# One broadcast VectorE multiply per output tile in an expert-dispatch kernel that copies and scales rows

## The chip, the cores and the metric

The kernel runs on one core of a Trainium2 chip. The metric is the device time of the whole program in microseconds (us); each run is one execution, and the median of the runs is taken. Durations inside the kernel come from one profiled execution.

Of the core's engines three issue or compute here: VectorE (DVE in the profile) and ScalarE (ACT) multiply, and SyncE (SP), ScalarE and GpSimd (POOL) issue transfers. The transfers themselves are carried by 16 DMA engines, which all three queues share. HBM is the memory off the core; SBUF is the memory on the core, with 128 partitions.

## The reference

Each of 16 x 1024 tokens has a row of 512 fp32 numbers and two weights. The output holds the row twice, once times each weight. The expert indices aren't used.

```python
batch, seq, hidden, n_experts, k = 16, 1024, 512, 8, 2

def reference(x, expert_indices, expert_weights):
    x_expanded = x[:, :, np.newaxis, :].repeat(k, axis=2)
    weights = expert_weights[..., np.newaxis]
    return (x_expanded * weights).astype(np.float32)
```

The input is 33.5 MB and the output 67.1 MB, all fp32; every input row is read once and every output row written once.

## The kernel before

**Tiles.** The 16,384 tokens are 128 tokens per partition over 128 partitions. They are cut into six load tiles: five of 24 tokens per partition (6.29 MB, 48 KB in each partition) and a last one of 8 (2.10 MB). The output of a load tile is made in pieces of `TO = 12` tokens per partition: two outputs for each of the first five load tiles (6.29 MB each) and one of 8 tokens (4.19 MB) for the last. So there are six loads, numbered 0 to 5, and eleven outputs, numbered 0 to 10.

**Buffers.** The pool of `x_tile` has two buffers, and so has the pool of `o_tile`. A third output can be made only when the first of the two before it has landed in HBM, and a third load can be issued only when the first tile has been read by its last multiply. All weights have one tile, `w_tile` (256 numbers per partition), filled at the start by six small loads from GpSimd's queue (line 54).

**Queues.** Loads are issued from ScalarE's queue (`load`, line 75), the first two at the very start and load i+2 behind the multiplies of load tile i (line 109). ScalarE also multiplies, and its instructions run in the order in which they are issued, so a load stands behind ScalarE's multiplies of its tile. Outputs are issued from SyncE's queue (line 105), which does nothing else; each waits for the multiplies that fill its buffer.

**Multiplies.** For each token and each of its two weights one instruction multiplies a block of 128 partitions x 512 numbers by one weight per partition. With `c` the column of the weight, the ones with `c % 3 == 2` go to ScalarE (line 90) and the others to VectorE (line 96): in a 12-token output 8 of the 24 on ScalarE and 16 on VectorE. The order on each engine is the order of the program; a tile framework puts in the waits.

Of the kernel before, what the change touches and what calls it, by code (L numbers as in the profile page):

```python
# [1 line left out]

# [4 lines left out]


@with_exitstack
def kernel(  # L10
    ctx: ExitStack,
    tc: tile.TileContext,
    x: bass.AP,
    expert_indices: bass.AP,
    expert_weights: bass.AP,
    out: bass.AP,
):
    nc = tc.nc

    batch, seq, hidden = x.shape  # L20
    k = expert_weights.shape[-1]
    P = nc.NUM_PARTITIONS
    ntok = batch * seq
    assert ntok % P == 0
    A_TOTAL = ntok // P

    f32 = mybir.dt.float32
    row = k * hidden
    TX = 24
    TO = 12  # L30

    groups = [[24], [24], [24], [24], [24], [8]]
    assert sum(sum(g) for g in groups) == A_TOTAL

    xf = x.rearrange("b s h -> (b s) h")
    of = out.rearrange("b s k h -> (b s) (k h)")
    wf = expert_weights.rearrange("b s k -> (b s) k")

    w_pool = ctx.enter_context(tc.tile_pool(name="w_pool", bufs=1))
    x_pool = ctx.enter_context(tc.tile_pool(name="x_pool", bufs=2))  # L40
    o_pool = ctx.enter_context(tc.tile_pool(name="o_pool", bufs=2))

    w_tile = w_pool.tile([P, A_TOTAL * k], f32)

    def rows(of_all, done, T):
        return of_all[done * P : (done + T) * P, :].rearrange(
            "(p a) n -> p (a n)", a=T
        )

    weights = []  # L50
    for group in groups:
        weights.append((sum(n for _, n in weights), sum(group)))
    for at, T in weights:
        nc.gpsimd.dma_start(out=w_tile[:, at * k : (at + T) * k], in_=rows(wf, at, T))  # L54

    tiles = []
    done = 0
    for group in groups:
        T = sum(group)
        a0 = 0  # L60
        for n in group:
            tiles.append((done, T, a0, n))
            a0 += n
        done += T

    loaded = []

    def load(i):
        if i >= len(tiles):
            return  # L70
        done, T, a0, n = tiles[i]
        x_tile = x_pool.tile([P, TX * hidden], f32)
        cols = rows(xf, done, T)[:, a0 * hidden : (a0 + n) * hidden]
        for lo, hi in [(0, P)]:
            nc.scalar.dma_start(out=x_tile[lo:hi, : n * hidden], in_=cols[lo:hi, :])
        loaded.append(x_tile)

    for i in range(2):
        load(i)
    for i, (done, T, a0, n) in enumerate(tiles):  # L80
        x_tile = loaded[i]
        outr = rows(of, done, T)
        for t in range(n):
            if t % TO == 0:
                o_tile = o_pool.tile([P, TO * row], f32)
            for kk in range(k):
                c = (done + a0 + t) * k + kk
                o = t % TO * row + kk * hidden
                if c % 3 == 2:
                    nc.scalar.mul(  # L90
                        out=o_tile[:, o : o + hidden],
                        in_=x_tile[:, t * hidden : (t + 1) * hidden],
                        mul=w_tile[:, c : c + 1],
                    )
                    continue
                nc.vector.tensor_scalar(  # L96
                    out=o_tile[:, o : o + hidden],
                    in0=x_tile[:, t * hidden : (t + 1) * hidden],
                    scalar1=w_tile[:, c : c + 1],
                    scalar2=None,  # L100
                    op0=mybir.AluOpType.mult,
                )
            if (t + 1) % TO == 0 or t + 1 == n:
                at = t // TO * TO
                nc.sync.dma_start(  # L105
                    out=outr[:, (a0 + at) * row : (a0 + t + 1) * row],
                    in_=o_tile[:, : (t + 1 - at) * row],
                )
        load(i + 2)

# [1 line left out]
_INS = ['x', 'expert_indices', 'expert_weights']  # L112
_OUTS = [((16, 1024, 2, 512), 'float32')]


# [23 lines left out]
```

## Time and profile before

| | value |
|---|---|
| time, median of 3 runs | 241.27 us (240.94 to 241.39) |
| time of the profiled execution | 241.42 us |
| its span, first to last instruction | 239.7 us |
| bytes read from and written to HBM in it | 33.69 MB and 67.11 MB |
| VectorE multiplies (line 96) | 171, mean 479 ns, 16 of them back to back in 6.43 us |
| ScalarE multiplies (line 90) | 85, mean 708 ns, 8 of them back to back in 5.01 us |
| first load: issued, first multiply | 0.73 us, 19.33 us |
| first output issued | 25.84 us |
| last output issued, last landing seen | 218.79 us, 238.36 us |

The span counts from the first instruction to the last on the core. The profiled execution's own time is 1.7 us above its span. Below, a digit row cuts the span in 40 slices and gives the busy share of each in tenths (9 is 90% or more). In the chain of work that ended last, each piece is followed back to what released it; its lines hold the start, the length and the work. In a timeline line the first two numbers are start and length in us, then engine, line, operation, tiles and count, and in brackets the idle time before it and what ended it. A "q" behind an engine's name is its queue. A multiply's length is longer than the distance to the next one, since successive ones overlap.

### The profile page before, as it was taken

The page shows a single profiled execution, that of the slowest core. Times are in us where ns is not written, and L with a number is a line of the kernel's source. Part 1 is how long each engine was busy: PE and PEld are TensorE (multiplying, and loading weights), DVE is VectorE, ACT ScalarE, POOL GpSimd, SP SyncE. Part 2 cuts the span into 40 slices and gives each one's busy share as a digit, 9 for nine tenths or more (in the row PEclk, how much of TensorE's full clock was granted, in tenths as well). Part 3 has the DMA queues.
Part 4 walks back from the last instruction along what each step waited for, and adds up shares of the span by engine and source line. Part 5 has one row for each costly group of instructions (what it writes and reads, how often), then busy time and mean ns, then how long its engine had stood idle before and what let it go on. Part 6 is the DMA issues. An engine that isn't in the chain of part 4 may idle for free.

```text
span 239.7 us, 366 instructions
## 1 busy us (share of the span) xinstructions
DVE 68.6 (29%) x171; ACT 54.5 (23%) x86; POOL 3.5 (1%) x10
## 2 busy tenths in 40 slices
DVE  0007930000820820820055028003705406425000
ACT  0007900000800800800052016003505206122000
POOL 5000000000000000000000000000000000000000
DMA  7999999999999999999999999999999999999894
GB/s 262 468 442 408 402 394 402 492 410 410 451 451 402 436 468 410 418 476 418 402 459 443 402 443 453 418 427 459 418 402 459 407 459 451 394 451 459 388 432 175
DMA packets 2642, 100.81 MB, mean 421 GB/s; under 512 B 368, under 2 KB 464, under 8 KB 464
## 3 DMA queue, kind: packets, MB, share of 16 engines
q1 hardware_dynamic: 1584, 67.11, 64.7%
q10 hardware_dynamic: 864, 33.55, 33.2%
q0 software_dynamic: 192, 0.13, 0.2%
q14 instruction: 2, 0.02, 0.0%
HBM read 33.69 MB, written 67.11 MB: 421 GB/s over the span
## 4 chain that ended last, share of the span: by engine, by line
DMA 75%; DVE 15%; issue 0%; DVEq 0%; SPq 0%
DMA out_dram<-o_tile 67%; DVE o_tile L96 15%; DMA x_tile<-in_x_dram 8%; DVEq L134 0%; DVEq L96 0%; SPq L105 0%
## 5 line engine op out<-in xcount | busy, mean ns | idle before, releaser
L96 DVE TENSOR_SCALAR o_tile<-x_tile,w_tile 128x512 f32<-128x512 f32 x171 | 68.6, 479 | 150.1 <-DMA out_dram<-o_tile 130.8
L90 ACT ACTIVATE o_tile<-x_tile,w_tile 128x512 f32<-128x512 f32 x85 | 53.2, 708 | 143.7 <-DMA out_dram<-o_tile 143.7
L90 ACT ACT_TABLE_LOAD x1 | 1.3, 1283 | 19.3 <-DMA x_tile<-in_x_dram 19.3
L54 POOL DMA_DIRECT2D w_tile<-in_expert_weights_dram x6 | 3.3, 557 | 0.8 <-PEq L134 0.8
L123 POOL MEMSET const-float32-0.0<- 128x1 f32 x1 | 0.1, 99 | 0.2 <-issue 0.2
L123 POOL MEMSET const-bfloat16-1.0<- 128x1 bf16 x1 | 0.1, 102 | 0.0
L123 POOL MEMSET const-float32-1.0<- 128x1 f32 x1 | 0.1, 99 | 0.0
L123 POOL MEMSET const-uint8-127<- 128x1 uint8 x1 | 0.1, 99 | 0.0
## 6 DMA issues: line engine op xcount, KB each, us to landing
out_dram<-o_tile SPq DMA_DIRECT2D x10, 6144.0 KB, 34.0
x_tile<-in_x_dram ACTq DMA_DIRECT2D x5, 6144.0 KB, 33.9
out_dram<-o_tile SPq DMA_DIRECT2D x1, 4096.0 KB, 19.6
x_tile<-in_x_dram ACTq DMA_DIRECT2D x1, 2048.0 KB, 23.5
w_tile<-in_expert_weights_dram POOLq DMA_DIRECT2D x5, 24.0 KB, 14.8
w_tile<-in_expert_weights_dram POOLq DMA_DIRECT2D x1, 8.0 KB, 22.7
```

What stands on the lines that cost most here:

```text
L54: nc.gpsimd.dma_start(out=w_tile[:, at * k : (at + T) * k], in_=rows(wf, at, T))
L90: nc.scalar.mul(out=o_tile[:, o : o + hidden], in_=x_tile[:, t * hidden : (t + 1) * hidden], mul=w_tile[:, c : c + 1],)
L96: nc.vector.tensor_scalar(out=o_tile[:, o : o + hidden], in0=x_tile[:, t * hidden : (t + 1) * hidden], scalar1=w_tile[:, c : c + 1], scala ...
L123: nc = _bacc.Bacc("TRN2", target_bir_lowering=False, num_devices=1)
```

## The change

The loop over the two weights and its two kinds of instruction are taken out. Instead, when the last token of an output tile is reached, one VectorE `tensor_tensor` makes the whole output: its first input is the `x_tile` rows of these tokens, each repeated for the two weights by a step of 0; its second input is the weights of these tokens, each repeated over 512 numbers by a step of 0; its output is the whole `o_tile`, 12 x 2 x 512 = 12,288 numbers per partition (8,192 in the last output). ScalarE multiplies nothing any more and only issues the loads. Buffers, tile sizes, the queues and the places of the loads and of the outputs in the program stay.

```diff
         for t in range(n):
             if t % TO == 0:
                 o_tile = o_pool.tile([P, TO * row], f32)
-            for kk in range(k):
-                c = (done + a0 + t) * k + kk
-                o = t % TO * row + kk * hidden
-                if c % 3 == 2:
-                    nc.scalar.mul(
-                        out=o_tile[:, o : o + hidden],
-                        in_=x_tile[:, t * hidden : (t + 1) * hidden],
-                        mul=w_tile[:, c : c + 1],
-                    )
-                    continue
-                nc.vector.tensor_scalar(
-                    out=o_tile[:, o : o + hidden],
-                    in0=x_tile[:, t * hidden : (t + 1) * hidden],
-                    scalar1=w_tile[:, c : c + 1],
-                    scalar2=None,
-                    op0=mybir.AluOpType.mult,
-                )
             if (t + 1) % TO == 0 or t + 1 == n:
                 at = t // TO * TO
+                m = t + 1 - at
+                c = (done + a0 + at) * k
+                shape = [P, m, k, hidden]
+                nc.vector.tensor_tensor(
+                    out=o_tile[:, : m * row].rearrange(
+                        "p (t k h) -> p t k h", k=k, h=hidden
+                    ),
+                    in0=x_tile[:, at * hidden : (t + 1) * hidden]
+                    .rearrange("p (t o h) -> p t o h", o=1, h=hidden)
+                    .to_broadcast(shape),
+                    in1=w_tile[:, c : c + m * k]
+                    .rearrange("p (t k o) -> p t k o", k=k, o=1)
+                    .to_broadcast(shape),
+                    op=mybir.AluOpType.mult,
+                )
                 nc.sync.dma_start(
                     out=outr[:, (a0 + at) * row : (a0 + t + 1) * row],
                     in_=o_tile[:, : (t + 1 - at) * row],
```

## The prediction

> **What bounds the kernel now.** I read the page's busy shares, slices and chain first, then the chain in order of time and the timeline of the last tiles, to see what covers what.
>
> ```profile
> span 239.7 us, 366 instructions
> DVE 68.6 (29%) x171; ACT 54.5 (23%) x86; POOL 3.5 (1%) x10
> DMA  7999999999999999999999999999999999999894
> HBM read 33.69 MB, written 67.11 MB: 421 GB/s over the span
> DMA 75%; DVE 15%; issue 0%; DVEq 0%; SPq 0%
> ```
>
> VectorE works 29% of the span and ScalarE 23%, while the DMA engines are full in nearly every slice. The chain puts 15% on VectorE, but the DMA row shows no dip in those stretches: while VectorE fills one output buffer, the other one is on its way out. So the transfers bound the kernel, and VectorE matters only if it takes longer than what the DMA engines still have queued.
>
> How long that cover is shows where no load is in flight:
>
> ```profile
> 199.80 6.42 DVE L96 TENSOR_SCALAR o_tile<-x_tile,w_tile 128x512 f32<-128x512 f32 x16 [11.20 <-DMA out_dram<-o_tile]
> 206.29 12.84 SPq L105 DMA_DIRECT2D out_dram<-o_tile  x2
> 214.28 4.45 DVE L96 TENSOR_SCALAR o_tile<-x_tile,w_tile 128x512 f32<-128x512 f32 x11 [8.06 <-DMA out_dram<-o_tile]
> ```
>
> I number the eleven outputs 0 to 10 and the six loads 0 to 5. VectorE starts at 199.80 because output 7 has landed, and at 214.28 because output 8 has. Between them only outputs move: one output of 6.29 MB takes 14.48 us alone, 434 GB/s. Output 9 is issued at 206.29, so today there is about 8 us to spare. Where a load moves too, the cover is longer: in the whole timeline VectorE starts at 97.05 and 122.43 on two successive landings with load 3 beside them, 25.4 us.
>
> The start and a handover:
>
> ```profile
> 19.22 0.03 issue
> 19.25 0.02 DVEq L96
> 19.27 0.06 issue
> 19.33 6.43 DVE o_tile L96 x16
> 25.76 0.02 issue
> 25.78 0.02 SPq L105
> 25.80 0.04 issue
> 25.84 34.83 DMA out_dram<-o_tile
> 60.66 0.03 issue
> 60.69 0.05 DVEq L96
> 60.74 0.05 issue
> 60.79 6.43 DVE o_tile L96 x16
> ```
>
> Landing to first VectorE work is 0.13 us (60.66 to 60.79), VectorE's end to the issue of the output 0.08 us (25.76 to 25.84). From the trace's records of single packets come two more: load 0 is issued at 0.73 and its first packet starts at 1.75, so 1.02 us; its last packet ends at 18.67 and the landing is seen at 19.22, so 0.55 us.
>
> **The change, part by part.** *Removed from ScalarE:* 85 multiplies and a table load, 54.5 us. They lie beside VectorE's work: in each tile 8 x 626 ns (8 in 5.01 us) against VectorE's 16 x 402 ns (16 in 6.43 us), and VectorE ends last. Nothing comes off the path.
>
> *Loads on ScalarE's queue:* the same six, in the same order. Loads 2 to 5 still wait for the last reader of their x_tile, which was VectorE and stays VectorE (issues at 85.43 on SP and 85.44 on ACT in one go). Only their time moves with C, below. SP's outputs and POOL's six weight loads keep their order and number.
>
> *VectorE:* 16 instructions per 12-token tile become one with 12,288 results; in the 8-token tile one with 8,192. Its length C replaces 6.43 us. No row shows such an operation, so I bound it. Today's VectorE pace for all 24 rows is 24 x 0.402 = 9.65 us. At ScalarE's pace it is 24 x 0.626 = 15.0 us. Twice the VectorE time, since two streams are read where one was, is 19.3 us. Between: an instruction's fixed part, paid once now, may be near the 0.10 us of the 128x1 memsets in the trace; 0.30 us of stream doubled is 24 x 0.60 = 14.4 us. I take the mean of 9.65, 14.4 and 15.0, 13.0 us, and keep 9.65 and 19.3 as ends. VectorE's busy time would be 10.67 tiles x 13.0 = 139 us, 58% of the span: the engine is still not the bound by its sum.
>
> [...] No run here shows the operation yet.
>
> *What C does at a handover.* When output j lands, VectorE makes output j+2, and the DMA engines live on output j+1 and on any load. Load and odd output are issued together, so when an even output is made (2, 4, 6, 8) both are in flight, 25 us or more of cover: free. When an odd one is made (3, 5, 7, 9), the load is about done and only the even output, 14.48 us, is left: four thin handovers. Output 10 takes 8/12 x 13.0 = 8.7 us under output 9's 14.48: free. At the start output 0 is made from 19.33 with only load 1 in flight: a fifth one. Output 1 is made while output 0 moves: it is issued about 45.4, output 0 ends about 48: free.
>
> The gap at a thin handover: from the landing it takes 0.13 + C + 0.08 + f until new packets move, with f the delay from issue to first packet; the cover ends 14.48 - 0.55 = 13.93 after the landing. Gap = C + f - 13.72. For f I have 1.02 us (load 0, idle engines) and, from the packet records, 3.65 us (load 3, issued at 85.44, first packet 89.09, behind other packets). At a thin handover the engines run dry, so I take 1.2, near the first. With C = 13.0 the gap is 0.48 us; break-even is C = 12.7 at f = 1.02. The start by itself: output 0 issued at 19.33 + 13.0 + 0.08 = 32.4, first packet 33.6; load 1 ends about 18.67 + 14.48 = 33.15: gap 0.45, the same. After a gap the wait is for the next landing: everything behind moves by it, for the DMA engines never get idle time back.
>
> Sum: 5 x 0.48 = 2.4 us. The profiled execution took 241.42 us (span 239.7 and 1.7 around it): 243.8 us. It lies 0.15 above the median of the three runs, less than I can tell; 0.2% (0.5 us) is what a measurement here tells from no change.
>
> **The rivals.**
> *The cover holds, no loss.* If C is below 12.7 us no gap opens at any thin handover, and the time stays 241.3. For it: today's pace gives 9.65; also, a load packet that trails behind its output adds cover. Against it: two streams are read. A gain can go with it: outputs start 6.6 us later, so the end of load 1 runs unmixed. The slices from 18 to 42 us moved 408, 402, 394 and 402 GB/s against 434 later; if all of that came back, 24 us x 32/434 = 1.8 us, so 239.6 at best. Only part of it can, since the first slices are slow with loads alone.
> *VectorE sets the pace of the thin handovers.* At C = 14.4 the gap is 1.9 us, the sum 241.4 + 9.4 = 250.8; at 15.0 it is 2.5 and 253.8; at 19.3 it is 6.8 and 275. For it: ScalarE needs 626 ns per row with one stream; against: VectorE does one row in 402.
> *A slow restart.* With f = 3.65 and C = 13.0 each gap is 2.9 us: 241.4 + 14.6 = 256. For it: three loads had to wait so long; against: they stood behind packets of another queue, which at a dry handover are gone. A middle f of 2.2 gives 1.5 each, 248.8.
> *The change doesn't do what it says:* the instruction order of the changed kernel shows eleven TensorTensor on VectorE and no multiply on ScalarE, so I give this nothing.
>
> **How the numbers follow.** Small gaps (C about 13, f 1.0 to 1.8): 0.60, 242 to 247, likeliest 243.8. Cover holds: 0.22, of it 0.14 within 0.2% and 0.08 faster. VectorE sets the pace: 0.12. Slow restart: 0.06. Slower: 0.60 + 0.12 + 0.06 = 0.78. The range goes from 240.8, no change and a little of the gain, to 250.5, which takes in the middle restart and C up to 14.4.
>
> **What would show it.** In the profile after: VectorE's one line with 11 instructions near 13.0 us for the 12-token ones, busy near 139 us; ScalarE near nothing; the first output issued near 32.4 us; the DMA row below 9 near 33 us and before the issues of outputs 3, 5, 7 and 9 (near 90, 134, 178 and 212 us) and full elsewhere; one output alone still 14.5 us. A mean under 12.7 us with a full DMA row would prove the first rival; gaps at every landing the second; a dry stretch well over 1.2 us between issue and first packet the third. The prediction is wrong if the slices between the handovers move less than 434 GB/s, which no term here has.

## The result, and the profile after

| | before | after |
|---|---|---|
| time, median | 241.31 us (4 runs, 240.94 to 241.39) | 247.45 us (4 runs, 246.77 to 247.66) |
| ratio to before, 95% interval | | 1.0256 [1.0239, 1.0273] |
| profiled execution, its span | 241.42 us, 239.7 us | 247.66 us, 245.9 us |

The change makes the kernel 2.6% slower. The direction was forecast; the forecast of 243.8 us priced the loss at 2.4 us, and it is 6.1 us.

The page of the changed kernel: its span, busy times, the DMA row (a slice is 6.1 us here), the GB/s moved in each slice, the chain's shares, and the multiply's group (busy, mean ns, idle before).

```profile
span 245.9 us, 108 instructions
DVE 138.2 (56%) x11; POOL 3.5 (1%) x10
DMA  7999999999999988899899999999998989989895
GB/s 265 487 408 405 472 400 400 384 376 408 456 416 432 464 384 264 384 440 456 384 472 424 384 344 424 456 440 424 424 432 341 469 384 426 512 384 512 384 426 256
DMA 63%; DVE 30%; issue 0%; DVEq 0%
L91 DVE TENSOR_TENSOR o_tile<-x_tile,w_tile 128x12288 f32<-128x12288 f32 (+1 forms) x11 | 138.2, 12570 | 91.1 <-DMA out_dram<-o_tile 71.9
```

VectorE is busy twice as long, 138.2 us for 68.6, and still only 56% of the span; its share of the chain went from 15% to 30%. The DMA row now has dips, and the slice from 92 to 98 us moved 264 GB/s. That is around the issue of output 3, one of the odd outputs.

The timeline there; ahead of it stands the line of fill 4 from the kernel before:

```profile
97.05 6.43 DVE L96 TENSOR_SCALAR o_tile<-x_tile,w_tile 128x512 f32<-128x512 f32 x16 [11.69 <-DMA out_dram<-o_tile]
```

```profile
61.95 46.74 SPq L103 DMA_DIRECT2D out_dram<-o_tile  x3
80.83 12.96 DVE L91 TENSOR_TENSOR o_tile<-x_tile,w_tile 128x12288 f32<-128x12288 f32 x1 [18.91 <-DMA out_dram<-o_tile]
93.82 0.37 ACTq L75 DMA_DIRECT2D x_tile<-in_x_dram  x1
95.37 12.96 DVE L91 TENSOR_TENSOR o_tile<-x_tile,w_tile 128x12288 f32<-128x12288 f32 x1 [1.58 <-DMA out_dram<-o_tile]
```

Fill 3 runs from 80.83 to 93.79 us; load 3 and output 3 are issued at 93.82, and output 2, the only cover, has landed by 95.37. VectorE idles 1.58 us ahead of fill 4, where it idled 11.69 us before. So the handover is as thin as the prediction drew it. Now the same core's windows (length, VectorE, GpSimd, clock, DMA share, GB/s), first across this handover, then behind it, across the handover at output 5, and behind that:

```profile
90.00:102.00 12.00, 10.42 (x2) 0.00 (x0) 1.00 0.85 315
104.00:122.00 18.00, 4.33 (x1) 0.00 (x0) 1.00 1.00 431
138.00:148.00 10.00, 8.27 (x2) 0.00 (x0) 1.00 0.98 354
150.00:170.00 20.00, 3.87 (x1) 0.00 (x0) 1.00 1.00 433
```

In the third line the DMA engines are busy 98% of the time and yet move 354 GB/s, against 433 in the fourth. Time without transfers hardly explains that: the transfers themselves were slower there. The prediction had no such term. (A window counts a packet's bytes where it starts, so short windows are rough; the packet records below settle it.)

The trace records single packets: one packet is one partition's 48 KB, and takes 1.815 us on one of the 16 DMA engines in 1,738 of the 1,920 records of this size before and in 1,523 of them after. Two sums over these records, averaged over the 16 engines, account for the span. *Dry* is time in which an engine has no packet; *slow* is what its packets take beyond 1.815 us (scaled for the smaller ones). The end is that of the last packet. Records overlap a little, so a dry time down to -0.4 is zero.

```
us per engine            first 20 us   from 20 us to 4 before the end   last 4 us
                         dry   slow     dry    slow                      dry
before                   2.32  0.97    -0.17   1.33                      1.34
after                    2.41  0.85     3.13   5.62                      0.07
```

The span grew by 6.2 us: dry stretches in the middle +3.3, slow packets +4.3, and at the end 1.3 back. After each dry stretch all engines begin together: the first packets of output 3 start within 0.27 us (94.64 to 94.91) on the 16 engines, where before they were spread over 3.6 us; those of outputs 0, 5 and 7 start within 0.39, 0.32 and 0.29 us, before within 3.8, 3.4 and 2.4. The end got better since the engines now finish together too: the last packets of the 16 engines end within 0.16 us, where before they ended over 1.9 us. The first packets are also where the slow time sits: the first packet of output 3 on each engine took 2.05 to 2.93 us, the first of load 3 1.815 to 3.48 us, and the second ones at most 1.91.

On none of the five thin handovers did all 16 engines stand still. The last packet of output 2 ends at 94.91 us, and the first of output 3 starts at 94.64, 0.27 us earlier (0.39, 0.31, 0.29 and 0.15 us at outputs 0, 5, 7 and 9); at 93.5 us one engine is still at work. The dry time is that of the engines that finish an output early, here from 92.28 us on.

### The profile page after: what moved, and what is told of

It reads as the page before. It is cut to its first block, busy times and chain, and to the rows that moved or that the text cites. A ratio compares the mean times of both kernels' runs of the same rounds, so it can differ in the third digit from the quotient of the medians.

```text
span 245.9 us, 108 instructions
## 1 busy us (share of the span) xinstructions
DVE 138.2 (56%) x11; POOL 3.5 (1%) x10
## 4 chain that ended last, share of the span: by engine, by line
DMA 63%; DVE 30%; issue 0%; DVEq 0%
DMA out_dram<-o_tile 55%; DVE o_tile L91 30%; DMA x_tile<-in_x_dram 7%; DVEq L91 0%
## 5 line engine op out<-in xcount | busy, mean ns | idle before, releaser
L91 DVE TENSOR_TENSOR o_tile<-x_tile,w_tile 128x12288 f32<-128x12288 f32 (+1 forms) x11 | 138.2, 12570 | 91.1 <-DMA out_dram<-o_tile 71.9
## 6 DMA issues: line engine op xcount, KB each, us to landing
out_dram<-o_tile SPq DMA_DIRECT2D x1, 4096.0 KB, 15.3
```

Of the source, the lines that this page charges most:

```text
L91: nc.vector.tensor_tensor(out=o_tile[:, : m * row].rearrange("p (t k h) -> p t k h", k=k, h=hidden), in0=x_tile[:, at * hidden : (t + 1) * ...
```

## The experiments

Each time is compared with runs of the kernel before on the same chip, whose medians were 241.05 to 241.32 us.

**e1: one-row multiplies on VectorE for everything.** In the kernel before, the branch for ScalarE goes.

```diff
-                if c % 3 == 2:
-                    nc.scalar.mul(
...
-                    continue
                 nc.vector.tensor_scalar(
```

> All 24 rows of an output are made by VectorE's one-row multiplies, ScalarE multiplies nothing; the two-stream instruction is not used. Theory (what costs is the length of the fill, C, against the 13 us or so that one output in flight covers): C is 24 x 0.402 = 9.65 us, about 3 us below the cover, no dry stretch, no slow first packets, time 240.5 to 242, as before. Rival (taking the multiplies from ScalarE, so that its queue holds loads alone, is what costs): 246 to 248.

Measured: 242.79 us, ratio 1.0063 [1.0041, 1.0085]. A fill took 9.59 us. There is no dry stretch (-0.05) and 2.93 us of slow packets, of which 1.6 are new. So the loss is not that ScalarE's queue holds loads alone: that is so here too, and three quarters of the loss is gone. At 0.8 us over the expected range, it isn't all gone. The profiled execution, to which the dry and slow times belong, was the slowest of the eight, 244.16 us: in it 0.9 us of slow packets came at 134 to 170 us and 0.4 us at 176 to 190, where loads 4 and 5 joined, with hardly any dry time ahead of them (0.16 us at 178), and 2.56 us of dry time in the last 4 us.

**e2: two thirds of a fill by the two-stream multiply.**

```diff
+                v = m * 2 // 3
-                shape = [P, m, k, hidden]
+                shape = [P, v, k, hidden]
...
+                for u in range(v, m):
+                    for kk in range(k):
+                        nc.scalar.mul(...)
```

> The two-stream multiply makes two thirds of each output (8 of 12 tokens), ScalarE the last third with one-row multiplies beside it. Theory (length against cover): C falls from 12.97 to 8.7 us, the time goes back to 240.5 to 242. Rival (a two-stream multiply disturbs the transfers while it runs, or an output made by one long instruction is worse than by 24): with two thirds of the instruction left at least half of the loss stays, 244 or more, and there are slow packets while it runs.

Measured: 242.28 us, ratio 1.0054 [1.0024, 1.0084]; dry -0.25, slow 1.79. VectorE is busy with two-stream multiplies for 92.3 us, and there are neither dry stretches nor, with 0.5 us, many new slow packets. So it isn't the instruction as such that costs, but the length of the fill.

**e3: loads behind the odd outputs, on their queue.**

```diff
-            nc.scalar.dma_start(out=x_tile[lo:hi, : n * hidden], in_=cols[lo:hi, :])
+            q = nc.scalar if i < 2 else nc.sync
+            q.dma_start(out=x_tile[lo:hi, : n * hidden], in_=cols[lo:hi, :])
```

> As the changed kernel, but loads 2 to 5 are issued from the queue of the outputs, behind the odd output, so that they don't share the DMA engines with it but come after it. Theory: each odd fill then has a load besides an output as cover, and no two queues start together: neither dry stretches nor slow first packets after the first output, time 239.5 to 242 although C stays 12.97. Rival (the long fill itself costs, about 1 us at each of the odd fills, whatever is queued): 246 to 248.

Measured: 244.37 us, ratio 1.0115 [1.0093, 1.0136]: half of the loss. The cover did what was expected, dry time is gone but for 0.5 us at the start. What was not expected is 2.69 us of slow packets, at 60 to 64 and 74 to 79 us and hardly later, and 2.6 us of dry time in the last 4 us: the engines end at different times. Two queues starting together are not needed for slow packets.

**e4: loads issued later.** ScalarE first writes seven blocks, made from the finished output, into the free x_tile; the output is unchanged.

```diff
+        if i + 2 < len(tiles):
+            for u in range(7):
+                nc.scalar.mul(
+                    out=x_tile[:, u * hidden : (u + 1) * hidden],
+                    in_=o_tile[:, u * hidden : (u + 1) * hidden],
+                    mul=2.0,
+                )
         load(i + 2)
```

> As the changed kernel, but ScalarE copies 7 blocks (about 4.5 us) out of the finished output into the free x_tile before it issues loads 2 to 5; C and the odd outputs' issue stay. Theory (the slow first packets come from two queues starting together on engines that have run dry, some 5 us in all): the outputs start alone with packets of 1.8 us as output 0 did, the load joins a running queue; dry time stays, slow time goes, 242 to 244.5. Rival (a load's first packets are slow whenever no load was moving, whatever else runs): slow time stays, 246.5 to 248. Rival (only the dry stretches count): no change or worse by the later loads, 247 to 249.

Measured: 245.21 us, ratio 1.0151 [1.0131, 1.017], between theory and rival; dry 2.26, slow 3.96. The dry time is 0.6 us at the start and 1.9 us ahead of output 9; ahead of outputs 3, 5 and 7 there is none. Behind the dry start at 32 us the slow packets stayed (1.7 us at 49 to 60), although load 2 came 3.8 us after output 1. So the idea that two queues must start together fell. Load 3 joined a running output, with no dry stretch ahead, and had none. Load 4 joined one too, and 1.0 us of slow packets came at 136 to 150 us and 0.6 us more up to 162. A dry stretch ahead is thus not needed for slow packets: without one they were thinner, spread over 26 us, but summed up to as much.

**e5 and e8: two that went another way than meant.** e5 shortened fills 0, 3, 5, 7 and 9 as e2 did, e8 was e3 with fill 0 shortened in that way.

```diff
-                v = m * 2 // 3
+                j = 2 * i + t // TO
+                v = m * 2 // 3 if j in (0, 3, 5, 7, 9) else m
```

> As the changed kernel, but fills 0, 3, 5, 7 and 9 have their last third made by ScalarE (C = 8.7 us), the other six keep the full two-stream multiply (12.97 us). Theory (only these five fills are thin): the time falls as far as with all fills short, 241.5 to 243. Rival (each long fill costs its share): about half of the gain, 244 to 246.

> As the run with loads behind the outputs (e3), but the first output alone has its last third made by ScalarE, so that it is issued before load 1 is through and the engines don't run dry at the start. In e3 the slow packets (about 2 us) came at 60 to 64 and 74 to 79 us, after a start in which all 16 DMA engines had begun together. Theory (slow packets come when all engines turn from writing to reading or back in one moment, which a dry stretch brings about): without the dry start these slow packets go, 241 to 243. Rival (a turn between outputs and loads on one queue is slow in itself): they stay, 243.5 to 245.

Measured: 253.38 us, ratio 1.051 [1.0479, 1.054], and 252.87 us, ratio 1.0476 [1.0451, 1.0501]. In these two programs the framework put output 1 ahead of output 0 on SyncE's queue: the first issue waits for VectorE's second fill, and only the second one for ScalarE, which of these two has a part in output 0 alone. The page of e5:

```profile
DMA  7999906899999899999999898999999999899994
GB/s 267 485 391 436 446 0 188 376 438 438 438 438 438 376 493 384 344 407 446 431 399 478 384 485 384 470 407 470 407 454 423 425 410 478 384 485 391 454 418 188
```

No packet starts in the slice from 31 to 38 us, since the first output is issued at 40.48: load 1 ends at 33.1 us and the first packet of an output starts at 41.3. The dry time in the middle is 9.0 us in e5 and 8.8 in e8. So neither answers the question put to it. But e8 has the slow packets of e3 again, at the first two turns behind its dry start (0.8 us at 66 to 73 and 1.1 at 83 to 89), and only 0.5 us in all later.

**e6: the even fills short.** As e5, with `j in (1, 2, 4, 6, 8)`; here the outputs go out in order.

> The counterpart: fills 1, 2, 4, 6 and 8 short (8.7 us), fills 0, 3, 5, 7 and 9 full (12.97 us). Theory: nothing is gained, the thin fills stay as long as they were, 246 to 248. Rival (each long fill costs its share): 244 to 246.

Measured: 247.73 us, ratio 1.0267 [1.0222, 1.0311]; dry 3.02, slow 5.77, both as in the changed kernel. Cutting 4.3 us off each of five fills gains nothing. The handover at output 3 is the one of the changed kernel, with nearly the same idle time behind it, 1.53 us for 1.58:

```profile
81.24 12.96 DVE L93 TENSOR_TENSOR o_tile<-x_tile,w_tile 128x12288 f32<-128x12288 f32 x1 [16.70 <-DMA out_dram<-o_tile]
94.23 10.59 SPq L114 DMA_DIRECT2D out_dram<-o_tile  x2
94.29 0.34 ACTq L75 DMA_DIRECT2D x_tile<-in_x_dram  x1
95.72 5.01 ACT L109 ACTIVATE o_tile<-x_tile,w_tile 128x512 f32<-128x512 f32 x8 [34.87 <-DMA out_dram<-o_tile]
95.73 8.69 DVE L93 TENSOR_TENSOR o_tile<-x_tile,w_tile 128x8192 f32<-128x8192 f32 x1 [1.53 <-DMA out_dram<-o_tile]
```

**e9: the odd fills short, by one-row multiplies.**

```diff
+                if 2 * i + t // TO in (0, 3, 5, 7, 9):
+                    for u in range(m * k):
+                        nc.vector.tensor_scalar(...)
+                else:
                     nc.vector.tensor_tensor(
```

> Fills 0, 3, 5, 7 and 9 by VectorE's 24 one-row multiplies (9.6 us), the other six by the two-stream multiply (12.97 us); in e5 the same fills were short, but its first two outputs went out in the wrong order, both at 40.5 us. Theory (only these five fills are thin): as with all fills at 9.6 us (e1, 242.8): 241.5 to 243.5, no dry stretch, under 0.5 us of slow packets at each odd output. Rival (each long fill costs its share): 244.5 to 246.

Measured: 242.39 us, ratio 1.0046 [1.0032, 1.006]; dry -0.23, slow 1.70. With six two-stream fills left, five of them of full length, it is as fast as with no full-length fill (e1, e2). The same place:

```profile
77.95 9.59 DVE L92 TENSOR_SCALAR o_tile<-x_tile,w_tile 128x512 f32<-128x512 f32 x24 [12.43 <-DMA out_dram<-o_tile]
87.57 19.94 SPq L113 DMA_DIRECT2D out_dram<-o_tile  x2
87.58 0.37 ACTq L75 DMA_DIRECT2D x_tile<-in_x_dram  x1
94.19 12.96 DVE L101 TENSOR_TENSOR o_tile<-x_tile,w_tile 128x12288 f32<-128x12288 f32 x1 [6.65 <-DMA out_dram<-o_tile]
```

Output 3 goes out at 87.57 and output 2 lands at 94.19, so 6.6 us of cover are left. e6 and e9 together show which fills are thin.

**e7: longer fills.** Two tokens of each fill are multiplied twice.

```diff
+                nc.vector.tensor_tensor(
+                    out=o_tile[:, : 2 * row].rearrange(
...
                 nc.vector.tensor_tensor(
                     out=o_tile[:, : m * row].rearrange(
```

> As the changed kernel, with 2 of the 12 tokens multiplied once more ahead of each fill: each fill 15.2 us, the first 17.4. Theory: all five thin fills are past break-even, so each us more is a us more of dry stretch: 4 x 2.2 + 4.4 = 13 us more, 257 to 262. Rival (the loss is mostly slow first packets, which don't grow with C): 2 to 6 us more, 249 to 254.

Measured: 259.61 us, ratio 1.0773 [1.0748, 1.0798], 12.2 us over the changed kernel where 13 were expected. Its timeline at output 3:

```profile
83.18 2.29 DVE L91 TENSOR_TENSOR o_tile<-x_tile,w_tile 128x2048 f32<-128x2048 f32 x1 [15.48 <-DMA out_dram<-o_tile]
85.50 12.96 DVE L104 TENSOR_TENSOR o_tile<-x_tile,w_tile 128x12288 f32<-128x12288 f32 x1
98.38 2.28 DVE L91 TENSOR_TENSOR o_tile<-x_tile,w_tile 128x2048 f32<-128x2048 f32 x1
98.49 0.33 SPq L116 DMA_DIRECT2D out_dram<-o_tile  x1
```

The fill takes 15.3 us, and VectorE has no idle time ahead of the next one: output 2's last packet ends at 97.30, before output 3 is issued at 98.49, and the next packet starts at 99.32: for 2.0 us nothing moves on any engine. Dry time went from 3.13 to 14.34 us and slow time stayed, 5.62 to 5.64. The dry part grew with C much as the prediction's formula says. The slow part didn't grow with the stretches; ahead of output 9, where no load comes, there are 2.2 us of dry time and only 0.1 us of slow packets.

**e10: e3 without the dry start.** Fill 0 alone by one-row multiplies.

> Loads behind the outputs as in e3, and fill 0 alone by one-row multiplies (9.6 us), so that output 0 is issued while load 1 still moves; e8 was meant to be this, but its first two outputs went out in the wrong order and the engines were dry for 9 us. Theory (slow packets come when all 16 engines turn between writing and reading in one moment, after a dry stretch has put them in step): the slow packets of e3 at 60 to 79 us go, 241 to 243. Rival (a turn from outputs to a load on one queue is slow in itself, whenever): they stay, 243.5 to 245.

Measured: 243.15 us, ratio 1.0076 [1.0059, 1.0093], at the border of both ranges. The packets decide: of the slow time at 58 to 82 us 0.3 us is left, where e3 had 1.8 (the whole middle: dry -0.29, slow 1.64; e3 had 2.69). In the windows from 58 to 82 us, e3 first and e10 second, the columns as above:

```profile
58.00:82.00 24.00, 16.76 (x2) 0.00 (x0) 1.00 1.01 406
```

```profile
58.00:82.00 24.00, 16.83 (x2) 0.00 (x0) 1.00 1.01 430
```

Both stretches are full, and e3 moves 24 GB/s less. The transfers come in the same order and on the same queues in both, with the same turns from output to load and back; only fill 0 and with it the dry start differ. Most of e10's remaining loss lies at the end: 2.70 us dry in the last 4, and 2.2 us between span and profiled time (243.20 and 241.0) where the kernel before has 1.7.

**e11: the kernel before, with loads behind the outputs.** The diff of e3, on the kernel before.

> The kernel before, with loads 2 to 5 issued behind the odd outputs on their queue. Theory: the transfers bound both and no fill is thin, 240.5 to 242. Rival (one queue for both moves fewer bytes, or turns cost): 243 to 245, which would say that e3 kept its loss for that reason and not for the dry start.

Measured: 243.14 us, ratio 1.0078 [1.0061, 1.0095], which falls in the rival's range, though hardly by slow packets (1.77) and not by a dry middle (-0.23). The last 4 us have 2.83 us of dry time against 1.34: the engines end less evenly, as in e10. This is there with C = 6.4 us, so the long fill isn't needed for it. That the shared queue makes it isn't shown: e1, with two queues, ended with 2.56 us and e9 with 2.08.

**e12: three smaller output buffers.**

```diff
-    TO = 12
+    TO = 8
-    o_pool = ctx.enter_context(tc.tile_pool(name="o_pool", bufs=2))
+    o_pool = ctx.enter_context(tc.tile_pool(name="o_pool", bufs=3))
```

> As the changed kernel, with outputs of 8 tokens and three output buffers in place of 12 and two (the same memory): a fill is 8.7 us and two outputs of 4.19 MB, 19.3 us, are in flight beside it; output 0 is issued near 28 us, before load 1 is through. Theory (length of the fill against its cover): no dry stretch, 240.5 to 242.5, with VectorE as busy as in the changed kernel, 138 us. Rival (the two-stream multiply's busy time or its stream is what costs): 245 or more.

Measured: 240.79 us (10 runs, 240.48 to 241.55), ratio 0.9988 [0.9978, 0.9998]. From its page, and then from its timeline:

```profile
span 238.9 us, 127 instructions
DVE 138.8 (58%) x16; POOL 3.5 (1%) x10
DMA  7999999999999999999999999999999999999995
```

```profile
18.82 34.50 DVE L91 TENSOR_TENSOR o_tile<-x_tile,w_tile 128x8192 f32<-128x8192 f32 x4 [18.82 <-DMA x_tile<-in_x_dram]
27.54 190.49 SPq L103 DMA_DIRECT2D out_dram<-o_tile  x16
87.89 8.69 DVE L91 TENSOR_TENSOR o_tile<-x_tile,w_tile 128x8192 f32<-128x8192 f32 x1 [1.01 <-DMA out_dram<-o_tile]
```

VectorE is as busy as in the changed kernel, sometimes with 1 us between fills, and the DMA row is full: two outputs lie beside each fill, and the first leaves at 27.54. The two-stream multiply with its cover restored costs nothing. (Its instructions and its packets are shorter here, 8,192 numbers and 32 KB; that this alone would do it isn't excluded, but e9, with five fills of full length, has hardly any loss in the middle either.) By a hair, 0.1%, this is the fastest of all kernels run.

The dry and slow times of the middle part, for all of them side by side:

```
kernel                                   dry     slow    time, us
before                                  -0.17    1.33    241.3
after                                    3.13    5.62    247.5
e1  all fills 9.6 us                    -0.05    2.93    242.8
e2  all fills 8.7 us                    -0.25    1.79    242.3
e3  loads behind outputs                 0.24    2.69    244.4
e4  loads later                          2.26    3.96    245.2
e5  odd fills short, outputs exchanged   9.02    3.82    253.4
e6  even fills short                     3.02    5.77    247.7
e7  all fills 15.2 us                   14.34    5.64    259.6
e8  e3, outputs exchanged                8.83    2.90    252.9
e9  odd fills short                     -0.23    1.70    242.4
e10 e3, fill 0 short                    -0.29    1.64    243.2
e11 before, loads behind outputs        -0.23    1.77    243.1
e12 three buffers of 8 tokens           -0.37    1.60    240.8
```

## Why the prediction was right in its mechanism and wrong in its size

*What bounds the kernel, and where.* Right. The transfers bound it, VectorE costs only at thin handovers, and these are the fills of outputs 0, 3, 5, 7 and 9: e6 and e9 show it by shortening the one half or the other. At output 9, where no load follows, the changed kernel lost nothing: from 219 to 221 us dry and slow time are 0.0 us.

*The length C.* 13.0 us was taken between 9.65 and 19.3; it is 12.96 us, and 8.69 us for 8,192 results. The 13.0 was the mean of three paces, and that it hit so closely is luck:

```profile
206.04 12.96 DVE L91 TENSOR_TENSOR o_tile<-x_tile,w_tile 128x12288 f32<-128x12288 f32 x1 [6.86 <-DMA out_dram<-o_tile]
220.59 8.69 DVE L91 TENSOR_TENSOR o_tile<-x_tile,w_tile 128x8192 f32<-128x8192 f32 x1 [1.60 <-DMA out_dram<-o_tile]
```

With both inputs repeated by steps of 0, each added result took 1.04 ns (2.28 us for 2,048 results in e7, 5.49 for 5,120 in e2, 8.69 for 8,192 and 12.96 for 12,288). In place of 24 one-row multiplies, which take 9.59 us in e1, 0.78 ns per result, one long instruction is slower.

*The handover, f.* Taken 1.2 us; the first packets came 0.82 to 0.86 us after the issues of outputs 0, 3, 5 and 7, and 0.91 after that of output 9. The slow-restart rival, in its form of a long f, was wrong: the packets didn't start late, they took long.

*The dry time.* 5 x 0.48 = 2.4 us was forecast. The stretches were 0.7 us at the start, 1.9 ahead of output 3, 0.4 ahead of 5 and 0.35 ahead of 7, and nothing ahead of 9: 3.3 us in the middle. 1.3 us came back at the end, where the engines now finish together; the prediction held that idle time never comes back. Net 2.0, close to 2.4, but that is luck. With C = 12.96 and f = 0.84 as measured, the formula C + f - 13.72 gives 0.08 us per handover and 0.4 us in all. It is made for the last engine, and that one didn't run dry: output 2's last packet ended at 94.91, output 3's first started at 94.64, and so it was at outputs 0, 5, 7 and 9. What ran dry were the engines that had finished earlier, by 2.6 us ahead of output 3 and 1.1 ahead of 5 and 7, and the formula has no term for that. Its slope is confirmed by e7, 11.2 us of dry time where 13 were forecast for the added length.

*The step that failed.* The sum ended with "5 x 0.48 = 2.4 us": a handover was priced by the time in which nothing moves, and everything that moves was taken at 434 GB/s. The runs put a second term there, which the prediction left at nothing. Behind the dry stretches the first packets of a load and an output that meet take up to 3.5 us instead of 1.815 (1.4, 1.5, 1.6 and 0.6 us per engine at the meetings of loads 2 to 5), and the middle lost 4.3 us more by slow packets than before, more than by the dry time. The four meetings sum to 5.1 us; 0.7 us less was lost at 20 to 40 us, where load 1 now ran without output 0 beside it (0.24 us of slow packets for 0.97), a part of the gain that the first rival had named. The prediction said that slices between the handovers below 434 GB/s would make it wrong. They do move less, for some 6 us each at load 2, the first load behind the dry start, and behind the dry stretches at outputs 3 and 5, and for 3 us at output 7: 324 GB/s at 46 to 56 us, 315 at 90 to 102, 354 at 138 to 148 and 339 at 183 to 190. No row of the trace of before gave this price, but one hinted at it: the slices from 18 to 42 us at 394 to 408 GB/s, behind the start, which I read as a possible gain.

*What is shown and what isn't.* That the fill's length against its cover makes the loss is shown by e1, e2, e6, e7, e9 and e12. That a dry stretch brings the slow packets that follow it is shown by e3 against e10 (same order, same queues: 1.8 us with the dry start, 0.3 without) and fits e9 and e12, which have the two-stream multiply but no dry stretch in the middle. It isn't their only source: without one, 0.9 us came at load 4 in e1 and 1.6 us at load 4 in e4, thinner and over some 30 us, and what sets their size wasn't found. That they come because the 16 engines turn between writing and reading in one moment fits the spreads (0.27 us after, 3.6 us before) and the fact that in e3 they appear 27 us behind the dry start, at the first turn; but no run put engines in step without a dry stretch, or the reverse, so this stays an inference.

## What to carry to other kernels

Where transfers bound, compare each producer's time not with the total but with what is in flight beside it at its thinnest place: here one output of 14.48 us against a fill of 12.96 plus about 1 us of handover, and engines that finished up to 2.6 us apart, so that the early ones ran dry. At that edge the price was more than the dry time itself, for behind it up to 1.6 us of slow transfers came at the next meeting of a load and an output. More, smaller buffers in the same memory restored the cover at no cost (e12, 240.8 us against 241.05).

## What the runs showed of the hardware that was not expected

- Behind a dry stretch, the first packets took up to 3.5 us instead of 1.815 where a load and an output met (2.05 to 2.93 on the 16 engines for output 3). On one queue they took up to 3.1 us at the first turn from output to load, 27 us behind the dry start (e3); output 0, alone behind the dry start, took 1.85 to 2.3 us.
- With a dry stretch late in the kernel (at output 7 or 9: the changed kernel, e4, e6, e7) the engines ended in step: 0.07 to 0.08 us of dry time in the last 4 us, against 1.34 before and 0.79 to 2.83 in the other runs.
- Two programs whose diffs left the outputs' order alone had outputs 0 and 1 exchanged on their queue by the framework, which cost about 9 us of dry time.
